# Weight differences in w_out: rows loaded from GpSimd's queue with longer leads, operations and stores one step apart

## The chip, the cores and the metric

The kernel runs on one core of one Trainium2 chip. A core has TensorE (PE: matmuls, into PSUM), VectorE (DVE), ScalarE (ACT) and GpSimd (POOL), and SyncE (SP), which here only issues transfers. ScalarE and GpSimd can issue transfers too; each of the three has a queue of its own, and an instruction that stands in an engine's stream holds up what comes behind it there. The metric is the device time of one execution in microseconds, as the median of the runs taken.

## The reference

One layer of a hybrid encoder, for a prompt of 2048 tokens and a batch of 8 x 16 sampled tokens. Cut to what matters:

```
h   = rms_norm(x, norm_g[0])
z   = h @ w_in                                  # 1024 -> 3592, split among the heads
att = rms_norm(band_attention(qa, ka, va), g_att)
mls = mlstm(qb, kb, vb, ib, fb) * sigmoid(ob)
mix = concatenate([att, mls], -1) @ w_out       # 1024 -> 1024
x   = x + rms_norm(mix, norm_g[1])
u   = rms_norm(x, norm_g[2]) @ w_up             # 1024 -> 5632
y   = conv3(u) ; gate, up = split(y, 2)
x   = x + rms_norm((gelu(gate) * up) @ w_down, norm_g[3])   # 2816 -> 1024
```

The outputs are both x, the attention's keys and values, the mLSTM state and the convolution's last rows. Everything is float32.

## The kernel before, in words

A float32 product is made of three matmuls over a high and a low part of both operands (`mm3`, L104 to L108). The two FFN products are done by a seven-product scheme for 2 x 2 blocks in place of eight: besides the blocks of a weight it needs sums and differences of them. For w_down these are the weight differences of this change. w_down is laid out as 11 units of 128 x 2048 (`NK` = 11), and a unit holds four blocks of 512 columns, called rows 0 to 3 here (the blocks B11, B12, B22, B21). `folds` (L1176) turns each unit into four differences and stores them to the DRAM tensor `wtd`, from which the FFN reads them later (L1379):

```
row 0 = row 1 - row 0
row 1 = row 2 - row 1
row 2 = row 0 - row 2      # of the new row 0
row 3 = row 3 + row 2      # of the new row 2
```

Each is one VectorE operation on 128 x 512 float32 values, in place in one of six slots of the pool `spare` (L58, L71). A new unit's rows take slots that rows of an earlier unit leave, so their load has to wait until the stores of those have landed.

The stages follow one another: projections by w_in with attention and mLSTM worked in between, then the w_out stage (`project`, L976), then the FFN. The w_out stage goes over 17 tiles of 128 tokens: prompt tiles 0 to 7, the sampled tokens, prompt tiles 8 to 15. The last attention and mLSTM units are still worked off beside tiles 0 to 7; from tile 8 on the first FFN rows are prepared (`h2_units`, L1077: square, rsqrt, scale, transpose), and at the end the first up-projection weights are loaded and differenced (L1336 to L1343). Per tile there are:

- `load` of the mixed row `mr` (SP), `norm`: square on ScalarE (L997), then `att_ms` and `att_rs` on GpSimd (L89, L95: mean square and its power -0.5), then scaling on VectorE (L999);
- `turn_rows`: eight transposes on TensorE into `mT_pt`, a rounded high part by ScalarE (L212) and the remainder by VectorE (L213), both into `mt`;
- two halves of 512 columns, each of 24 matmuls into `wo`, evacuated by VectorE (L1033, into `mx`) and ScalarE (L1035, sum of squares), with `wssq` after the first half and `n_ms`, `n_rs` after the second on GpSimd, then the residual on VectorE (L1045) and its store on SP (L1046).

`folds` is a generator that `project` calls after every fourth k of a half (L1026 to L1030): four calls a tile, 68 in all. A unit takes six. In its first call, the loads of rows 0 and 1 are issued from ScalarE's queue (L1188); in the third those of rows 2 and 3 (L1193); the fourth to sixth make the first three operations (L1203); the first call of the next unit makes the fourth (L1208) and issues all four stores from GpSimd's queue (L1210).

The order on each engine is drawn up by the framework's list scheduler, which runs the traced program against a timeline of its own. `keep_in_program_order`, which wraps every load, operation and store of `folds`, puts an instruction behind the one traced just before it on the same engine; instructions that are not wrapped, the FFN's among them, may be drawn ahead of it or behind.

Of the kernel before, what the change touches and what calls it, by code (L numbers as in the profile page):

```python
# [38 lines left out]
HALF = [384, 384, 320]  # L39
PAIRS = [[(((b[j], 0), (b[j + 3], 0)), j * P, P, f"{b[j]}") for j in range(3)] for b in FBLOCKS[:2]]  # L40
NK = NF // 2
UPS = []
WOUT_FOLDS = [("T", k) for k in range(NK)] + [("U", f) for f in UPS]
FAST = (0, 1, 2)
ORDERS = [[f for k in range(NK) for f in (k, k + NK)] if b in FAST else list(range(NF)) for b in range(3)]
B11, B12, B22, B21 = range(4)
# [5 lines left out]
def hymba_step(ctx: ExitStack, tc: tile.TileContext, I: dict, O: dict):  # L52
    nc = tc.nc
# [8 lines left out]
    def ps_mm(name):  # L62
        return psum.tile([P, 512], F32, tag="mm", name=name)
# [7 lines left out]
    def spare_tile(name):  # L71
        return spare.tile([P, 512], F32, tag="k", name=name)

    def dt_(shape, name):
        return dram.tile(shape, F32, tag=name, name=name)
# [12 lines left out]
    def mean_square(ms, ssq, n, eps=EPS):  # L88
        nc.gpsimd.tensor_scalar(ms, ssq, 1.0 / n, eps, op0=ALU.mult, op1=ALU.add)  # L89

    def rsqrt_mean(ssq, n, name, eps=EPS):
        ms = small.tile([P, 1], F32, tag="ms", name=name + "_ms")
        mean_square(ms, ssq, n, eps)
        rs = small.tile([P, 1], F32, tag="rs", name=name + "_rs")
        nc.gpsimd.tensor_tensor(rs, ms, nhalf[:, 0:1], op=ALU.pow)  # L95
        return rs
# [30 lines left out]
    wtd = [dt_([P, 2048], f"wtd{k}") for k in range(NK)]  # L127
    wsd = [dt_([P, 2048], f"wsd{f}") for f in range(NF)]
# [3 lines left out]
    def x_src(t):  # L132
        return I["x_sample"] if t == SAMPLE else I["x_prompt"][t * P:(t + 1) * P, :]
# [84 lines left out]
    def rows_tile(tag, shape, name, dtype=F32):  # L218
        if tag == "xr":
            return rows.tile(shape, dtype, tag="xr", name=name, bufs=2)  # L220
        return pa.tile(shape, dtype, tag=tag, name=name, bufs=1)
# [750 lines left out]
    def drain():  # L972
        while any([p_.step() for p_ in pipes]):
            pass

    def project(tiles):  # L976

        ss = [SimpleNamespace(t=t) for t in tiles]

        def load(s):  # L980
            t = s.t
            if t == 8:
                drain()
                open_ffn()
            s.m = rows_tile("xr", [P, D], f"mr{t}")
            if t == SAMPLE:
                for b in range(DB):
                    own = bass.AP(atts[b].tensor, atts[b].offset, [[512, DS], [DS * 512 + DA, HA], [1, DA]])
                    nc.sync.dma_start(s.m[b * DS:(b + 1) * DS, 0:512].rearrange("p (h d) -> p h d", h=HA), own)
                nc.sync.dma_start(s.m[:, 512:D], mixs)  # L990
            else:
                nc.sync.dma_start(s.m, mixd[t // 4][:, t % 4, :])

        def norm(s):
            mt = wpool.tile([P, 2112], F32R, tag="wh", name=f"mt{s.t}", bufs=2)
            ssq = small.tile([P, 1], F32, tag="ssq", name=f"assq{s.t}")
            nc.scalar.activation(mt[:, :512], s.m[:, :512], AF.Square, accum_out=ssq)  # L997
            rs = rsqrt_mean(ssq, 512, f"att{s.t}")
            nc.vector.tensor_scalar(s.m[:, :512], s.m[:, :512], rs, None, op0=ALU.mult)  # L999
            s.mt = mt[:, :2 * D].rearrange("p (a k n) -> p a k n", a=2, k=KT)  # L1000

        def turn_rows(s):
            rows_to_T(s.m, s.mt, 0, f"mT{s.t}", ps_mm if s.t < 8 else ps_big)

        fold, owed = folds(WOUT_FOLDS), [0.0]
        load(ss[0])
        norm(ss[0])
        yield 0.0, 0.3
        turn_rows(ss[0])
        load(ss[1])  # L1010
        yield 0.9, 1.2
        for n_, s in enumerate(ss):
            t = s.t
            nxt = ss[n_ + 1] if n_ + 1 < len(ss) else None
            if nxt:
                norm(nxt)
            mx = wpool.tile([P, 2112], F32, tag="wl", name=f"mx{t}", bufs=2)
            m, xr = mx[:, 0:D], mx[:, D:2 * D]
            nc.sync.dma_start(xr, x_src(t))
            for hf in range(2):  # L1020
                c = slice(hf * 512, hf * 512 + 512)
                acc = ps_mm(f"wo{t}_{hf}")
                for k in range(KT):
                    mm3(acc, s.mt[:, 0, k, :], s.mt[:, 1, k, :], wo[k][0][:, c], wo[k][1][:, c],
                        start=(k == 0), stop=(k == KT - 1))
                    if k % 4 == 3:  # L1026
                        owed[0] += 6 * len(WOUT_FOLDS) / 66
                        while owed[0] >= 1:
                            owed[0] -= 1
                            next(fold, None)  # L1030
                        yield 2.6, 0.5
                ssq = small.tile([P, 1], F32, tag="wssq", name=f"wssq{t}_{hf}")
                nc.vector.tensor_tensor(m[:, c], acc, g1[0][:, c], op=ALU.mult)  # L1033
                idle = m[:, 512:D] if hf == 0 else s.mt[:, 0, 0:4, :].rearrange("p k n -> p (k n)")
                nc.scalar.activation(idle, acc, AF.Square, accum_out=ssq)  # L1035
                if hf == 0:
                    ssa = ssq
                    mean_square(ssa, ssq, D)
                    if nxt:
                        turn_rows(nxt)  # L1040
                        if n_ + 2 < len(ss):
                            load(ss[n_ + 2])
                        yield 0.9, 1.2
            rs = rsqrt_mean(ssq, D, f"n1_{t}", ssa)
            nc.vector.scalar_tensor_tensor(xr, m, rs, xr, op0=ALU.mult, op1=ALU.add)  # L1045
            nc.sync.dma_start(x2d[t], xr)  # L1046
        for _ in fold:
            pass
# [8 lines left out]
    def open_ffn():  # L1057

        p1.close()
        ffn.p3 = ctx.enter_context(tc.tile_pool(name="p3", bufs=2, reuse_waits="tile"))  # L1060
        ffn.halo = ffn.p3.tile([P, 44, 2], F32, tag="halo", name="halo", bufs=1)
        nc.vector.memset(ffn.halo, 0.0)
        ffn.g2 = ffn.p3.tile([P, D], F32, tag="g2", name="g2", bufs=1)
        nc.sync.dma_start(ffn.g2, I["norm_g"][2:3, :].broadcast_to([P, D]))
        pipes[:] = [Pipe(h2_units(0, lead=6)), Pipe(iter([]))]
# [107 lines left out]
            nc.scalar.copy(hi, lo.bitcast(F32))  # L1173
            nc.vector.tensor_tensor(lo, lo.bitcast(F32), hi, op=ALU.subtract)

    def folds(units):  # L1176

        keep = tc.keep_in_program_order
        sub, plus = ALU.subtract, ALU.add
        ahead = None  # L1180
        for n_, (what, k) in enumerate(units):
            src, dst = (I["w_down"], wtd) if what == "T" else (I["w_up"], wsd)
            part = lambda d, x: d[k][:, x * 512:(x + 1) * 512]
            if ahead:
                ahead()
            q = [spare_tile(f"fold{what}{k}_{x}") for x in range(2)]
            for x in range(2):
                keep(nc.scalar.dma_start(q[x], part(src, x)))  # L1188
            yield
            yield  # L1190
            q += [spare_tile(f"fold{what}{k}_{x}") for x in (2, 3)]
            for x in (2, 3):
                keep(nc.scalar.dma_start(q[x], part(src, x)))  # L1193
            yield
            a, b, c, d = q
            if what == "T":
                ops = [(a, b, a, sub), (b, c, b, sub), (c, a, c, sub), (d, d, c, plus)]
                out = [a, b, c, d]
            else:
                ops = [(c, d, c, plus), (d, a, d, sub), (a, c, a, sub), (b, b, a, sub)]  # L1200
                out = [a, d, c, b]
            for o, x, y, op in ops[:3]:
                keep(nc.vector.tensor_tensor(o, x, y, op=op))  # L1203
                yield

            def ahead(out=out, dst=dst, k=k, last=ops[3]):
                o, x, y, op = last
                keep(nc.vector.tensor_tensor(o, x, y, op=op))  # L1208
                for i, t in enumerate(out):
                    keep(nc.gpsimd.dma_start(dst[k][:, i * 512:(i + 1) * 512], t))  # L1210
        ahead()

    GROUPS = ["va0", "qk0", "qk1", "va1", "qk2", "qk3", "qb0", "vo0", "qb1", "vo1", "qb2", "vo2", "qb3", "vo3"]
    SRC = {g: i for i, g in enumerate(["va0", "qk0", "qk1", "va1", "qk2", "qk3",
# [45 lines left out]
    for n_, (half, gi) in enumerate(seq):  # L1260
        wh, wl, _ = pend
# [5 lines left out]
        i = int(g[2])  # L1267
# [15 lines left out]
        if n_ == len(seq) - 1:  # L1283
            out = project([0, 1, 2, 3, 4, 5, 6, 7, SAMPLE, 8, 9, 10, 11, 12, 13, 14, 15])
# [3 lines left out]
        for u, (pe, dve) in enumerate(it):  # L1288
            ahead = []
# [191 lines left out]
    for b, tiles in enumerate(FBLOCKS):  # L1481
        last = b == len(FBLOCKS) - 1
# [136 lines left out]
        for fi, f in enumerate(ORDERS[b]):  # L1619
# [11 lines left out]
            a, d_, ec = ps_mm(f"ua{nm}"), ps_sm(f"ub{nm}"), ps_big(f"uec{nm}")  # L1631
            e, c = ec[:, 0:512], ec[:, 512:1024]
# [49 lines left out]
        ahead = Pipe(iter([]) if last else h2_units(b + 1, lead=2))  # L1682
        res = {}
        if fast:
# [96 lines left out]
            for p, (_, _, set_, onto) in enumerate(SEQUENCE):  # L1781
                for c in range(3):
# [19 lines left out]
                    for k in range(4 * c, min(4 * c + 4, NK)):  # L1802
                        i = 6 * p + k // 2
# [22 lines left out]
        for dh in range(2):  # L1826
# [56 lines left out]
            out = {j: evacuate(b, j, accs[j], dh) for j in order}  # L1883
# [113 lines left out]
```

## Time and profile before

| | |
|---|---|
| median of 3 runs | 2769.61 us |
| lowest and highest | 2769.04 and 2775.64 us |
| the profiled execution | 2760.67 us, of which its span 2759.0 us |
| mean granted TensorE clock | 0.994 |
| w_out stage, first to last w_out matmul | 1058.7 to 1337.2 us |
| bytes moved | 557.04 MB, mean 202 GB/s |

In the profile, a line such as L1210 is that of the kernel's text. PE is matmuls, PEld the loads of their stationary operand, which overlap. ACTq, SPq and POOLq are the engines' instruction streams where a transfer is issued or a semaphore waited for. A wait is told as "engine, tile, line <- who released it", with the total in us, the number of times and the longest. A row of the timeline has the start in us from the span's start, the duration, the instruction, and in brackets the idle time before it. A row of busy time by stretches has the stretch, its length, the busy us of each engine with its instructions, the granted clock, the DMA engines' busy share and GB/s.

### The profile page before, as it was taken

The numbers are of one execution on the slowest core, as the hardware profiler recorded it, in microseconds if no ns is written. First come the engines' busy times: TensorE is split into PE (matmuls) and PEld (weight loads), VectorE is DVE, ScalarE is ACT, GpSimd is POOL, SyncE is SP. The second block draws the span as 40 slices with busy tenths as digits, with TensorE's granted clock in tenths as the row PEclk, the third lists the DMA queues.
The fourth block names the chain that finished last, engine by engine and source line by source line (L and its number), as shares of the span: only waits on it lengthen the run. The fifth ranks groups of instructions, "written<-read, shape, count | busy, mean of one in ns | idle before, by whom it ended". The sixth has DMA issues, their size and how long they took to land.

```text
span 2759.0 us, 47858 instructions
## 1 busy us (share of the span) xinstructions
PE 2676.8 (97%) x16323; PEld 2506.6 (91%) x16323; DVE 1923.1 (70%) x3643; ACT 1458.3 (53%) x2961; POOL 695.8 (25%) x1353
## 2 busy tenths in 40 slices
PE   7999999999999998999899999999999999999998
PEld 7899999998899997877799997789999878999976
DVE  5344455646446567756799998758888876899966
ACT  4355545635346666533455556654554665555654
POOL 1000010211100002233355542023443212455401
PEclk9999999999999999999999999999999999999999
DMA  5534355547564456568866668767886777789885
GB/s 183 160 116 139 106 160 163 170 149 213 158 190 137 136 173 217 189 221 269 281 202 199 204 203 265 248 199 203 240 240 192 245 236 244 213 257 256 248 270 183
DMA packets 339987, 557.04 MB, mean 202 GB/s; under 512 B 62082, under 2 KB 168414, under 8 KB 339614
## 3 DMA queue, kind: packets, MB, share of 16 engines
q1 hardware_dynamic: 252846, 400.31, 47.0%
q0 software_dynamic: 41968, 108.30, 13.3%
q10 hardware_dynamic: 44928, 45.37, 5.1%
q8 instruction: 128, 2.10, 0.3%
q14 instruction: 117, 0.96, 0.1%
HBM read 389.77 MB, written 173.49 MB: 204 GB/s over the span
## 4 chain that ended last, share of the span: by engine, by line
PE 42%; DVE 4%; DMA 4%; issue 2%; ACT 1%; POOL 1%; DVEq 0%; SPq 0%; POOLq 0%; ACTq 0%
PE uec L106 5%; PE uec L107 5%; PE uec L108 5%; PE dn L108 3%; PE dn L106 3%; PE dn L107 3%; PE ua L108 3%; PE ua L106 2%; PE ua L107 2%; PE dnm L108 1%; PE dnm L107 1%; PE dnm L106 1%; PE ub L108 1%; PE ub L107 1%; PE ub L106 1%
## 5 line engine op out<-in xcount | busy, mean ns | idle before, releaser
L106 PE MATMUL uec<-B,wuh 128*128 128x384 f32 (+1 forms) x720 | 236.2, 328 | 5.7 <-DVE uu L1660 3.5
L107 PE MATMUL uec<-B,wuh 128*128 128x384 f32 (+1 forms) x720 | 235.4, 327 | 0.0
L108 PE MATMUL uec<-B,wul 128*128 128x384 f32 (+1 forms) x720 | 234.7, 327 | 0.0
L1324 ACT CAST wuh<-wu 128x512 fp32r<-128x512 f32 x255 | 141.6, 618 | 109.0 <-PE uec L107 107.6
L108 PE MATMUL dn<-wdh,al 128*128 128x512 f32 x462 | 185.3, 401 | 4.7 <-DVE al L1325 4.5
L1325 DVE TENSOR_TENSOR al<-ar,ah 128x768 fp32r<-128x768 f32 (+2 forms) x141 | 108.6, 780 | 116.0 <-ACT ah L1324 114.5
L106 PE MATMUL dn<-wdh,ah 128*128 128x512 f32 x462 | 183.0, 396 | 4.6 <-ACT ah L1324 2.9
L107 PE MATMUL dn<-wdl,ah 128*128 128x512 f32 x462 | 182.1, 394 | 0.0
L1324 ACT CAST ah<-ar 128x768 fp32r<-128x768 f32 (+2 forms) x141 | 96.2, 692 | 149.9 <-PE dnm L107 110.8
L1325 DVE TENSOR_TENSOR wul<-wu,wuh 128x512 fp32r<-128x512 f32 x255 | 164.5, 685 | 2.4 <-ACT wuh L1324 2.4
L407 DVE CUSTOM_DVE_ANT_0 tmp<-s,nb 128x640 f32<-128x640 f32 (+4 forms) x128 | 94.5, 738 | 94.0 <-PE s L397 92.5
L106 PE MATMUL vo<-wi_h,hT 128*128 128x256 f32 x544 | 155.6, 286 | 0.6 <-DVE mt L213 0.6
L108 PE MATMUL vo<-wi_h,hT 128*128 128x256 f32 x544 | 156.0, 287 | 0.0
L107 PE MATMUL vo<-wi_l,hT 128*128 128x256 f32 x544 | 155.2, 285 | 0.0
L1325 DVE TENSOR_TENSOR wdl<-wdr,wdh 128x512 fp32r<-128x512 f32 x231 | 145.4, 685 | 8.0 <-ACT wdh L1324 5.9
L106 PEld LDWEIGHTS uec<-B,wuh 128*128 128x128 f32 x720 | 135.3, 188 | 8.5 <-DVE uu L1660 4.3
L420 DVE TENSOR_TENSOR ptl<-pt,pth 128x640 fp32r<-128x640 f32 (+4 forms) x128 | 93.9, 738 | 60.8 <-ACT pth L419 59.8
L107 PEld LDWEIGHTS uec<-B,wuh 128*128 128x128 f32 x720 | 135.4, 188 | 0.2
L108 PEld LDWEIGHTS uec<-B,wul 128*128 128x128 f32 x720 | 135.4, 188 | 0.0
L1324 ACT CAST wdh<-wdr 128x512 fp32r<-128x512 f32 x231 | 127.4, 620 | 11.4 <-PE uec L107 7.3
L106 PE MATMUL qk<-hT,wi_h 128*128 128x384 f32 (+1 forms) x384 | 129.6, 337 | 3.6 <-ACT qk_st L238 2.8
L408 ACT ACTIVATE tmp<-tmp,mn 128x640 f32<-128x640 f32 (+4 forms) x128 | 97.6, 763 | 65.9 <-DVE mn L407 64.5
(426 smaller groups left out, 9227.8 us busy)
## 6 DMA issues: line engine op xcount, KB each, us to landing
wu<-in_w_up SPq DMA_DIRECT2D x220, 256.0 KB, 4.9
wu<-wsd SPq DMA_DIRECT2D x176, 256.0 KB, 5.0
wdr<-wtd SPq DMA_DIRECT2D x132, 256.0 KB, 4.8
wi_raw<-in_w_in SPq DMA_DIRECT2D x52, 512.0 KB, 4.0
wdr<-in_w_down SPq DMA_DIRECT2D x99, 256.0 KB, 4.7
wsd<-ws POOLq DMA_DIRECT2D x88, 256.0 KB, 4.8
ar<-ad_S SPq DMA_DIRECT2D x50, 384.0 KB, 5.5
kraw<-kTd SPq DMA_DIRECT2D x112, 128.0 KB, 3.0
```

Of the source, the lines that this page charges most:

```text
L106: nc.tensor.matmul(out, ah, bh, start=start, stop=False, skip_group_check=onto)
L107: nc.tensor.matmul(out, ah, bl, start=False, stop=False, skip_group_check=onto)
L108: nc.tensor.matmul(out, al, bh, start=False, stop=stop, skip_group_check=onto)
L407: nc.vector.tensor_tensor_reduce(o_, s_, b_, 1.0, 3e38, ALU.add, ALU.min, accum_out=mn)
L408: nc.scalar.activation(tmp[:, :n], tmp[:, :n], AF.Exp, bias=mn, scale=-1.0, accum_out=rsum[:, i % 4, hh:hh + 1])
L420: nc.vector.tensor_tensor(s.ptl[:, sl, qc], ptv, s.pth[:, sl, qc], op=ALU.subtract)
L1324: nc.scalar.copy(h, r)
L1325: nc.vector.tensor_tensor(l, r, h, op=ALU.subtract)
```

## The change

Loads are issued from GpSimd's queue instead of ScalarE's. The order within a unit becomes: loads of rows 0 and 1 in the unit's first call, of rows 2 and 3 in the fourth, the first and second operation in the fifth and sixth; the third operation in the next unit's first call, ahead of that unit's loads; stores of rows 0 and 1, then the fourth operation, in its second; stores of rows 2 and 3 in its third. The rate stays one call after every fourth k (`FOLD_RATE` = 1.0; 6 x 11 / 66 before). The branch for differences of w_up, which had no units, goes.

```diff
--- before.py
+++ after.py
@@ -39,8 +39,7 @@
 HALF = [384, 384, 320]
 PAIRS = [[(((b[j], 0), (b[j + 3], 0)), j * P, P, f"{b[j]}") for j in range(3)] for b in FBLOCKS[:2]]
 NK = NF // 2
-UPS = []
-WOUT_FOLDS = [("T", k) for k in range(NK)] + [("U", f) for f in UPS]
+FOLD_RATE = 1.0
 FAST = (0, 1, 2)
 ORDERS = [[f for k in range(NK) for f in (k, k + NK)] if b in FAST else list(range(NF)) for b in range(3)]
 B11, B12, B22, B21 = range(4)
@@ -1002,7 +1001,7 @@
         def turn_rows(s):
             rows_to_T(s.m, s.mt, 0, f"mT{s.t}", ps_mm if s.t < 8 else ps_big)
 
-        fold, owed = folds(WOUT_FOLDS), [0.0]
+        fold, owed = folds(), [0.0]
         load(ss[0])
         norm(ss[0])
         yield 0.0, 0.3
@@ -1024,7 +1023,7 @@
                     mm3(acc, s.mt[:, 0, k, :], s.mt[:, 1, k, :], wo[k][0][:, c], wo[k][1][:, c],
                         start=(k == 0), stop=(k == KT - 1))
                     if k % 4 == 3:
-                        owed[0] += 6 * len(WOUT_FOLDS) / 66
+                        owed[0] += FOLD_RATE
                         while owed[0] >= 1:
                             owed[0] -= 1
                             next(fold, None)
@@ -1173,42 +1172,46 @@
             nc.scalar.copy(hi, lo.bitcast(F32))
             nc.vector.tensor_tensor(lo, lo.bitcast(F32), hi, op=ALU.subtract)
 
-    def folds(units):
+    def folds():
 
         keep = tc.keep_in_program_order
         sub, plus = ALU.subtract, ALU.add
-        ahead = None
-        for n_, (what, k) in enumerate(units):
-            src, dst = (I["w_down"], wtd) if what == "T" else (I["w_up"], wsd)
-            part = lambda d, x: d[k][:, x * 512:(x + 1) * 512]
-            if ahead:
-                ahead()
-            q = [spare_tile(f"fold{what}{k}_{x}") for x in range(2)]
-            for x in range(2):
-                keep(nc.scalar.dma_start(q[x], part(src, x)))
+        live = {}
+
+        def load(k, xs):
+            for x in xs:
+                live[k, x] = spare_tile(f"fold{k}_{x}")
+                keep(nc.gpsimd.dma_start(live[k, x], I["w_down"][k][:, x * 512:(x + 1) * 512]))
+
+        def make(k, o, x, y, op):
+            keep(nc.vector.tensor_tensor(live[k, o], live[k, x], live[k, y], op=op))
+
+        def store(k, xs):
+            for x in xs:
+                keep(nc.gpsimd.dma_start(wtd[k][:, x * 512:(x + 1) * 512], live.pop((k, x))))
+
+        for k in range(NK + 1):
+            now, old = k < NK, k > 0
+            if old:
+                make(k - 1, 2, 0, 2, sub)
+            if now:
+                load(k, (0, 1))
             yield
+            if old:
+                store(k - 1, (0, 1))
+                make(k - 1, 3, 3, 2, plus)
             yield
-            q += [spare_tile(f"fold{what}{k}_{x}") for x in (2, 3)]
-            for x in (2, 3):
-                keep(nc.scalar.dma_start(q[x], part(src, x)))
+            if old:
+                store(k - 1, (2, 3))
             yield
-            a, b, c, d = q
-            if what == "T":
-                ops = [(a, b, a, sub), (b, c, b, sub), (c, a, c, sub), (d, d, c, plus)]
-                out = [a, b, c, d]
-            else:
-                ops = [(c, d, c, plus), (d, a, d, sub), (a, c, a, sub), (b, b, a, sub)]
-                out = [a, d, c, b]
-            for o, x, y, op in ops[:3]:
-                keep(nc.vector.tensor_tensor(o, x, y, op=op))
-                yield
-
-            def ahead(out=out, dst=dst, k=k, last=ops[3]):
-                o, x, y, op = last
-                keep(nc.vector.tensor_tensor(o, x, y, op=op))
-                for i, t in enumerate(out):
-                    keep(nc.gpsimd.dma_start(dst[k][:, i * 512:(i + 1) * 512], t))
-        ahead()
+            if not now:
+                break
+            load(k, (2, 3))
+            yield
+            make(k, 0, 1, 0, sub)
+            yield
+            make(k, 1, 2, 1, sub)
+            yield
 
     GROUPS = ["va0", "qk0", "qk1", "va1", "qk2", "qk3", "qb0", "vo0", "qb1", "vo1", "qb2", "vo2", "qb3", "vo3"]
     SRC = {g: i for i, g in enumerate(["va0", "qk0", "qk1", "va1", "qk2", "qk3",
```

## The prediction

> **What bounds the kernel now.** I read the page's busy shares first, then busy time by stretches, then the waits of the one stage that the change touches, then single tiles there. The first two lines of the page:
>
> ```profile
> span 2759.0 us, 47858 instructions
> ...
> PE 2676.8 (97%) x16323; PEld 2506.6 (91%) x16323; DVE 1923.1 (70%) x3643; ACT 1458.3 (53%) x2961; POOL 695.8 (25%) x1353
> ```
>
> TensorE is the bound: busy 2676.8 of 2759.0 us, so an edit off TensorE can give back at most the 82.2 us in which it idles, and only idle time that the edit's own work causes. The w_out stage runs from the first w_out matmul at 1058.7 us to the last at 1337.2. Busy time in it, in its second part (tiles 8 to 15, no attention left) and in a stretch near its end; columns are PE, PEld, DVE, ACT, POOL, then granted clock, DMA share, GB/s:
>
> ```profile
> 1058.70:1337.20 278.50, 260.44 (x1367) 217.31 (x1367) 178.07 (x326) 124.08 (x299) 84.50 (x162) 0.98 0.70 226
> 1202.00:1337.00 135.00, 122.48 (x567) 97.92 (x566) 76.31 (x103) 47.26 (x98) 46.00 (x87) 0.96 0.82 269
> 1306.00:1321.00 15.00, 11.36 (x53) 8.90 (x52) 4.15 (x7) 3.01 (x7) 5.07 (x9) 0.99 0.91 279
> ```
>
> TensorE idles 278.5 - 260.4 = 18.1 us here, 0.65% of the time: the ceiling of any gain in this stage. GpSimd is busy 30% of it, ScalarE 45%, VectorE 64%. What TensorE waited for between 1080 and 1345 us (total, times, longest):
>
> ```profile
> PE wo L108 <- DVE mt L213: 7.8, 2, 7.3
> PE ot L432 <- ACT pth L419: 3.5, 1, 3.5
> PE h2T_pt L1115 <- DVE x2r L1107: 3.1, 2, 2.9
> ```
>
> No row names a weight difference: the three largest waits are for the split of a transposed tile, an attention probability and a normalised FFN row. The difference tiles themselves (durations ns min/median/max, then first and last start):
>
> ```profile
> L1210 POOL DMA_DIRECT2D wtd<-foldT x44: 539/542/769, 1087.2 to 1335.1; - x44
> L1203 DVE TENSOR_TENSOR foldT<-foldT,foldT x33: 674/684/694, 1086.2 to 1329.6; 128x512 f32<-128x512 f32 x33
> L1188 ACTq DMA_DIRECT2D foldT<-in_w_down x22: 334/354/1647, 1049.1 to 1307.2; - x22
> L1193 ACTq DMA_DIRECT2D foldT<-in_w_down x22: 334/335/566, 1064.3 to 1317.3; - x22
> L1208 DVE TENSOR_TENSOR foldT<-foldT,foldT x11: 627/683/689, 1100.4 to 1332.1; 128x512 f32<-128x512 f32 x11
> ...
>   DMA foldT<-in_w_down: 0.4, 1
> ...
> DMA to landing us min/median/max: 2.6/5.2/10.6
> ```
>
> VectorE waited for a loaded row once, 0.4 us. The result has no hurry either; its first reader comes 367 us after the last store:
>
> ```profile
> L1379 SPq DMA_DIRECT2D wdr<-wtd x132: 319/320/1306, 1702.9 to 2720.8; - x132
> ```
>
> **The change part by part.** Counts stay: 44 loads, 44 VectorE operations, 44 stores. The generator is called 68 times in the stage (17 tiles, two halves, two calls each), every 278.5 / 68 = 4.1 us on average; the last 38 calls, from the sixth unit's first load on, fall into the 135 us of the second row above, one every 3.6 us. I reckon with the shorter step.
>
> *The loads leave ScalarE.* 44 issues of 0.334 to 0.354 us, 15 us of its queue, and this wait for a slot whose store had not landed; beside it stand TensorE's largest wait on ScalarE and the queue's own waits for a slot:
>
> ```profile
> ACT mx L1035 <- DMA wtd<-foldT: 5.0, 1, 5.0
> ...
> 1084.83 0.38 PE L432 MATMUL ot<-pth,vhl 128*128 128x256 f32 x1 [3.47 <-ACT pth L419]
> ...
> L1193 ACTq EVENT_SEMAPHORE  x14: 17/17/17, 1097.5 to 1316.8; - x14
> ```
>
> ScalarE idles 154 of 278.5 us, and TensorE's largest wait on it, 3.5 us, ends at 1084.8, before the first wait for a slot at 1097.5, so it cannot come from one. On the path: 0.
>
> *The loads come to GpSimd.* There is no row for such a load; the nearest is the store, 0.542 us. 44 x 0.542 = 23.8 us, which takes GpSimd from 84.5 to 108 of 278.5 us. As time it is hidden by GpSimd's idle 194 us; as delay it stands ahead of the small rsqrt operations (att_ms, att_rs, n_ms, n_rs) that gate the normalised rows. A pair puts 1.1 us in front of them. The slack is read at a late tile, in order of time on GpSimd, VectorE, TensorE:
>
> ```profile
> 1309.10 0.55 POOL L95 TENSOR_TENSOR att_rs<-att_ms,nhalf 128x1 f32<-128x1 f32 x1
> 1309.60 2.29 POOL L1210 DMA_DIRECT2D wtd<-foldT  x4
> ...
> 1309.68 0.49 DVE L999 TENSOR_SCALAR mr<-mr,att_rs 128x512 f32<-128x512 f32 x1 [0.71 <-POOL att_rs L95]
> ...
> 1313.99 1.03 PE L78 MATMUL mT_pt<-ident,mr 128*128 128x128 f32 x8
> ```
>
> The row is normalised at 1310.17 and transposed at 1313.99: 3.8 us cover one or two issues. Cost 0; without that cover 1.1 us a pair, 22 pairs, 24 us at the very most. How long the load itself takes from issue to landing:
>
> ```profile
> foldT<-in_w_down ACTq DMA_DIRECT2D x44, 256.0 KB, 5.8
> wtd<-foldT POOLq DMA_DIRECT2D x44, 256.0 KB, 5.2
> ```
>
> GpSimd's queue is not slower for 256 KB, so the nearest estimate for the load is 5.2 to 5.8 us. By the Trainium skill, DMA: Bandwidth & Descriptors, section Specifications, a DMA from GpSimd delivers its first byte after about 1 us and one from ScalarE after about 0.6: by that each load would land 0.4 us later, an estimate that the two medians here do not show (they differ the other way, load against store).
>
> *The leads.* Rows 0 and 1 are used four calls after their load instead of three, 14.4 against 10.8 us; row 2 stays at two calls (7.2 us), row 3 at four. Against a landing of 5.2 to 5.8 us all have cover, and the wait that could go is the 0.4 us shown. If a load is late all the same, VectorE stands, and behind it the evacuation L1033; but that one waits itself:
>
> ```profile
> DVE mx L1033 <- PE wo L108: 26.8, 10, 5.3
> ```
>
> So 0. Bounds: -0.4, and on the other side row 2 of all 11 units landing at the longest, 10.6 - 7.2 = 3.4 us late, 37.4 us of VectorE, of which 26.8 it stands idle today: +10.6.
>
> *Operations and stores one call apart.* VectorE does the same 0.684 us each. The stores no longer stand in one burst of four behind the last operation, so these waits of GpSimd's queue go:
>
> ```profile
> POOL wtd L1210 <- DVE foldT L1203: 5.5, 3, 3.2
> POOL wtd L1210 <- DVE foldT L1208: 4.8, 4, 2.8
> POOL wtd L1210 <- DVE ad L657: 2.5, 1, 2.5
> ```
>
> 12.8 us of GpSimd standing, none of which reaches a row of TensorE's waits: 0. In exchange, GpSimd's own loads of rows 2 and 3 must wait until the store of the previous unit's rows 0 and 1 has landed, a wait that ScalarE carried so far. What stands behind it is the same rsqrt chain. Two calls (7.2 us) lie between, against a median landing of 5.2: 0 at the median. The other end is the second rival.
>
> *The end.* The last two operations slip one call, the last into the final half tile, and the last pair of stores (1.1 us) behind the stage. The closing evacuation waits for TensorE anyway:
>
> ```profile
> 1337.11 0.69 DVE L1033 TENSOR_TENSOR mx<-wo,norm_row 128x512 f32<-128x512 f32 x1 [4.38 <-PE wo L108]
> ```
>
> 4.4 us of idle cover 0.68: 0, or +0.7 at most without it.
>
> *The 7.3 us stall.* It arises where four FFN differences (L1341) stand before the split L213 on VectorE and their input lands late, with the DMA share at 0.91:
>
> ```profile
> 1308.83 1.07 SPq L1336 DMA_DIRECT2D wu<-in_w_up  x1
> ...
> 1320.88 0.69 DVE L1341 TENSOR_TENSOR ws<-wu,wu 128x512 f32<-128x512 f32 x1 [9.51 <-DMA wu<-in_w_up]
> ...
> 1323.42 1.22 DVE L213 TENSOR_TENSOR mt<-mT_pt,mt 128x1024 fp32r<-128x1024 f32 x1
> ...
> 1324.69 0.79 PE L108 MATMUL wo<-wo,mt 128*128 128x512 f32 x1 [7.33 <-DVE mt L213]
> ```
>
> The differences' traffic crosses that load: four stores at 1309.6 and loads on either side. After the change a pair of stores (0.52 MB, 1.9 us at 279 GB/s) comes a little later, and the pair of loads of that unit comes later too, behind att_rs: -1.9 to +1.9, and I take 0, since the bytes stay.
>
> **Sum.** 0 on the path. The profiled execution took 2760.67 us, its span 2759.0 and 1.67 around it; the median of the runs shown, 2769.61, lies 8.94 above it. So 2760.7 + 0 + 8.9 = 2769.6.
>
> **Rivals.** *B, the tail untangles (faster).* The order on each engine is drawn up by the framework's list scheduler on its own estimate of time, and a moved difference can shift the FFN work among the tiles. If L213 comes ahead of L1341, and the h2T transposes a few matmuls later, 7.3 + 2.9 = 10.2 us go: 2759.4. For: both stalls are orders that the data did not keep. Against: nothing edited is one of the instructions concerned.
>
> *C, GpSimd stands for its slots (slower).* Pinned only behind the previous GpSimd instruction, the four issues can run up close to one another: store pair, store pair, load pair. Then the load waits the store's landing less three issues, and the rsqrt chain stands behind it. It decides from the point where that hold passes the 3.8 us of slack. In the later seven units the transfers of these tiles land so:
>
> ```profile
> DMA to landing us min/median/max: 3.4/6.2/10.6
> ```
>
> A median store holds 6.2 - 1.6 = 4.6 us, 0.8 beyond the slack; the longest 9.0, 5.2 beyond. Two of the seven at the longest and five at the median: 10.4 + 4.0 = 14.4, so 2784.0. For: 82% DMA share there. Against: in the trace of before GpSimd stood 12.8 us for stores without a trace on TensorE.
>
> *D, the leads do not grow.* Issue order, not the call, sets when a queue gets to a load; behind att_rs or wssq the extra call may vanish. Waits move by tenths: 2769.6, as forecast.
>
> *E, GpSimd's issue is held by VectorE.* The longest GpSimd issue of any kind is an accumulating one:
>
> ```profile
> L1446 POOL DMA_DIRECT2D x2d<-f x24: 865/892/2075, 1908.3 to 2534.0; - x24
> ```
>
> If each load took 2.08 instead of 0.54 us, a pair would come 3.1 us later, and ten holds at C's all-stage median (5.2 - 1.6 = 3.6) would reach 6.7, 2.9 over the slack: +29, 2798.6. By the Trainium skill, SBUF — State Buffer, section SBUF: two separate sides, GpSimd cannot write descriptors while VectorE holds the port pair that both share. The 44 stores, at 769 ns at most beside a VectorE 64% busy, speak against it.
>
> **Numbers.** Forecast 0.46, B 0.20, C 0.21, D 0.10, E 0.03. About 0.3% (8.3 us) is what a measurement of this kernel can tell from no change: faster 0.20 (B), slower 0.24 (C and E), same 0.56. The forecast's own range is 2767 to 2778 (the tail's 1.9 and the leads' 0.4 about the runs shown, 2769.04 to 2775.64). The full range goes from 2756, B with the wait of 3.5 for pth reordered away too, to 2786, C with the tail's 1.9; the leads' +10.6 lies inside. Outside are E and about a third of C and of B, 0.17.
>
> **What would show it.** Right: 44 loads from GpSimd near 0.54 us each, ScalarE's 5.0 us slot wait gone, TensorE's idle time in the stage near 18 us, with L213 and x2r still its largest releasers. B: the 7.3 us row missing. C: GpSimd's loads idling on stores of wtd, and TensorE waiting on a chain that ends in att_rs. E: a load's issue well over 1 us. The forecast falls if TensorE's idle time changes by more than 8 us in this stage, or at all in the FFN, whose instructions the change does not touch.

## The result, and the profile after

| | before | after |
|---|---|---|
| median of six runs each | 2770.92 us | 2757.14 us |
| lowest to highest | 2765.86 to 2775.64 us | 2753.62 to 2764.04 us |
| the profiled execution | 2760.67 us | 2753.91 us |

The ratio of after to before is 0.9955, with a 95% interval of 0.9942 to 0.9969: the change makes the kernel 0.45% faster, some 12 us. The forecast, no change, did not come: the time lies below its own range (2767 to 2778), inside the full range (2756 to 2786), and near that of rival B (2759.4).

The first two lines of the page of after:

```profile
span 2752.2 us, 47852 instructions
...
PE 2677.0 (97%) x16323; PEld 2504.0 (91%) x16323; DVE 1922.8 (70%) x3643; ACT 1457.1 (53%) x2961; POOL 731.5 (27%) x1397
```

Over the whole execution TensorE is busy as long as before, 2677.0 against 2676.8 us. The w_out stage shows what went: first the kernel before, from the first to the last w_out matmul and in a stretch near the end, then the same stage after. Both stage rows hold the same matmuls, 1413 of them. The columns are the stretch, its length, the busy us of PE, PEld, DVE, ACT and POOL, the granted clock, DMA share and GB/s:

```profile
1050.30:1337.00 286.70, 267.55 (x1413) 223.47 (x1412) 184.36 (x340) 129.78 (x312) 86.27 (x165) 0.98 0.71 229
1320.80:1327.60 6.80, 2.91 (x7) 2.33 (x8) 4.92 (x7) 1.70 (x4) 2.98 (x6) 0.50 0.88 269
```

```profile
1049.20:1321.10 271.90, 263.43 (x1413) 219.63 (x1412) 184.25 (x341) 130.05 (x314) 113.64 (x207) 1.00 0.74 241
```

The stage is 14.8 us shorter. TensorE idles 8.5 us in it instead of 19.2, which makes 10.7; the same matmuls take 4.1 us less. The granted clock of before is 0.50 in three places of the stage: for 3.4 us from 1085.3 and from 1221.8, and for 6.8 from 1320.8, each at one of the three waits that the prediction shows. After, it is full all through the stage. TensorE's waits of after in the stage (total, times, longest):

```profile
PE pt L77 <- DVE ptl L419: 1.7, 1, 1.7
PE h2T_pt L1114 <- DVE x2r L1106: 1.6, 2, 0.9
...
PE wo L107 <- DVE mt L212: 0.4, 1, 0.4
```

The three largest waits of before are gone or short: 7.3 us for the split of a transposed tile (L213) is 0.4, 3.5 for an attention probability (L419) is 0.3, and 2.9 for a normalised FFN row (L1107) is 0.9 (the line numbers of after are lower by one up to `folds`, and higher by three behind it). From the first w_out matmul to the first of the down projection, the profiled executions took 611.3 us before and 599.8 after, 11.5 less: 3.3 of the stage's 14.8 us are lost again between its end and that point (324.6 and 327.9 us). (The first w_out matmul of before is at 1050.3 us; the 1058.7 given ahead of the prediction is a later one.) Behind that point every engine has the same instructions in the same order in both kernels. It took 1097.4 and 1103.2 us; that 5.8 the other way is spread between executions, and it is why the profiled pair differs by 6.8 us only.

**The first place: the tail of the stage.** The timeline of before, rows beside those that the prediction shows:

```profile
1306.09 1.58 SPq L1336 DMA_DIRECT2D wu<-in_w_up  x3
1306.76 0.37 ACTq L1188 DMA_DIRECT2D foldT<-in_w_down  x1
1307.22 0.41 ACTq L1188 DMA_DIRECT2D foldT<-in_w_down  x1
...
1325.28 0.63 PE L106 MATMUL wo<-wo,mt 128*128 128x512 f32 x1
1325.71 0.63 PE L107 MATMUL wo<-wo,mt 128*128 128x512 f32 x1
```

And the timeline of after:

```profile
1298.42 1.59 SPq L1339 DMA_DIRECT2D wu<-in_w_up  x3
...
1300.68 0.62 SPq L1339 DMA_DIRECT2D wu<-in_w_up  x1
...
1301.49 0.55 POOL L94 TENSOR_TENSOR att_rs<-att_ms,nhalf 128x1 f32<-128x1 f32 x1
1301.99 1.32 POOL L1184 DMA_DIRECT2D fold<-in_w_down  x2
1303.30 1.08 POOL L1191 DMA_DIRECT2D wtd<-fold  x2
...
1306.31 0.69 DVE L1344 TENSOR_TENSOR ws<-wu,wu 128x512 f32<-128x512 f32 x1 [1.82 <-DMA wu<-in_w_up]
...
1310.46 0.40 PE L105 MATMUL wo<-wo,mt 128*128 128x512 f32 x1
```

The FFN's first differences (ws) need four blocks of w_up, loaded by SyncE three and one. Before, ScalarE sends two 256 KB loads for the differences of w_down beside the second and the third, ahead of the fourth, and ws starts 12.05 us after the fourth was issued (1308.83, 1320.88). After, GpSimd sends the same two loads behind att_rs, 1.3 us after the fourth, and ws starts 5.63 us after it. VectorE waits 1.82 instead of 9.51 us for it. ws still stands before the split on VectorE: the order was not mended, its input came sooner. TensorE's 7.33 us becomes 0.39. Behind the long stall its matmuls also started 0.43 us apart instead of 0.23, some 1.2 us in all over the seven starts up to 1327.76. This place is worth 7.33 - 0.39 + 1.2 = 8.1 us.

What the DMA engines moved from the issue of the fourth block to ws, before and then after (q1 is SyncE's queue, q10 ScalarE's, q0 GpSimd's; packets, MB, share of the engines' time):

```profile
DMA packets 2039, 3.74 MB, mean 309 GB/s; under 512 B 210, under 2 KB 722, under 8 KB 2039
...
q1 hardware_dynamic: 1382, 2.07, 52.2%
q0 software_dynamic: 320, 1.05, 23.4%
q10 hardware_dynamic: 337, 0.62, 21.4%
```

```profile
DMA packets 1163, 1.64 MB, mean 294 GB/s; under 512 B 82, under 2 KB 594, under 8 KB 1162
...
q1 hardware_dynamic: 1156, 1.61, 92.8%
q0 software_dynamic: 6, 0.02, 1.1%
```

The rate is about the same; the bytes are not. Before, the pair and all four stores of differences (1.05 MB, issued 0.8 us and more behind the block) were moved before ws could start; after, next to nothing of either. The trace does not tell how much of the delay is the stores' doing.

**The second place: 1084 us.** ScalarE's stream before and after:

```profile
1082.60 0.42 ACT L662 ACTIVATE mvo<-mvo 128x256 f32<-128x256 f32 x1 [2.04 <-DMA mvo<-vobd]
...
1083.35 0.33 ACTq L1188 DMA_DIRECT2D foldT<-in_w_down  x1
1083.51 0.67 ACT L419 CAST pth<-pt 128x640 fp32r<-128x640 f32 x1
```

```profile
1076.40 1.29 ACT L418 CAST pth<-pt 128x640 fp32r<-128x640 f32 x2 [0.26 <-PE ot L431]
...
1078.59 0.41 ACT L661 ACTIVATE mvo<-mvo 128x256 f32<-128x256 f32 x1
```

Before, the mLSTM's gate (mvo) stands ahead of the attention's cast (pth) in ScalarE's stream and waits there for its load; TensorE stands 3.47 us for pth. After, pth comes first and TensorE waits 0.3. Here the order on an engine did change, between two instructions that the change does not touch. Worth 3.2 us of idle time in the pair of profiles, and the stretch of half clock behind it.

**The third place: 1222 us.** TensorE's longest wait for a normalised FFN row (x2r) is 2.9 us before and 0.9 after. The row's square on ScalarE waits for the load of x2r there, 4.0 us before and 2.1 after; why that load comes sooner was not looked into. The three places make 12.1 us of idle time; other waits took 1.4 back.

**The differences themselves.** The tile's view in after:

```profile
L1184 POOL DMA_DIRECT2D fold<-in_w_down x44: 543/544/764, 1053.9 to 1312.7; - x44
L1187 DVE TENSOR_TENSOR fold<-fold,fold x44: 628/684/695, 1074.8 to 1321.0; 128x512 f32<-128x512 f32 x44
...
  DMA wtd<-fold: 11.4, 6
  DVE fold L1187: 11.1, 4
  DMA fold<-in_w_down: 3.0, 2
```

GpSimd's load costs 0.544 us, as estimated. VectorE waits 3.0 us for rows instead of 0.4, in spite of the longer leads. GpSimd stands 11.4 us for slots, a wait that ScalarE had.

### The profile page after: what moved, and what is told of

Same layout as the page of the kernel before. It is cut to its first block, busy times and chain, and to the rows that moved or that the text cites. A ratio compares the mean times of both kernels' runs of the same rounds, so it can differ in the third digit from the quotient of the medians.

```text
span 2752.2 us, 47852 instructions
## 1 busy us (share of the span) xinstructions
PE 2677.0 (97%) x16323; PEld 2504.0 (91%) x16323; DVE 1922.8 (70%) x3643; ACT 1457.1 (53%) x2961; POOL 731.5 (27%) x1397
## 3 DMA queue, kind: packets, MB, share of 16 engines
q0 software_dynamic: 45488, 119.84, 14.8%
## 4 chain that ended last, share of the span: by engine, by line
PE 43%; DVE 4%; DMA 3%; issue 1%; ACT 1%; POOL 0%; SPq 0%; DVEq 0%; POOLq 0%; ACTq 0%
PE uec L105 5%; PE uec L106 5%; PE uec L107 5%; PE dn L107 3%; PE dn L105 3%; PE dn L106 3%; PE ua L107 3%; PE ua L106 3%; PE ua L105 3%; PE dnm L107 1%; PE dnm L106 1%; PE ub L107 1%; PE dnm L105 1%; PE ub L105 1%; PE ub L106 1%
## 5 line engine op out<-in xcount | busy, mean ns | idle before, releaser
L419 DVE TENSOR_TENSOR ptl<-pt,pth 128x640 fp32r<-128x640 f32 (+4 forms) x128 | 93.6, 738 | 57.8 <-ACT pth L418 56.9
```

The source lines that it names most:

```text
L419: nc.vector.tensor_tensor(s.ptl[:, sl, qc], ptv, s.pth[:, sl, qc], op=ALU.subtract)
```

## The experiments

All were timed in five rounds against the kernel before on the same chip. The stalls are those of TensorE in one profiled execution of each, and the last column is its stretch from the first w_out matmul to the first of the down projection.

| version | ratio to before | interval | stall at the tail | stall for pth | stretch |
|---|---|---|---|---|---|
| before | 1 | | 7.3 | 3.5 | 611.3 |
| the change | 0.9955 | 0.9942 to 0.9969 | 0.4 | 0.3 | 599.8 |
| e1, change, loads on ScalarE | 0.9986 | 0.9976 to 0.9997 | 7.1 | 2.7 | 611.5 |
| e2, before, loads on GpSimd | 0.9963 | 0.9950 to 0.9976 | 0.4 | 0.3 | 601.8 |
| e3, no differences | 0.9932 | 0.9918 to 0.9946 | none | 0.3 | 588.8 |
| e4, before, 1.2 calls | 1.0015 | 1.0001 to 1.0028 | none | 3.8 | 612.9 |
| f1, change, loads on SyncE | 0.9998 | 0.9986 to 1.0010 | 3.1 | 3.9 | 612.3 |
| g1, before, rows 0, 1 on GpSimd | 0.9955 | 0.9941 to 0.9970 | 0.5 | 2.0 | 603.6 |
| g2, before, rows 2, 3 on GpSimd | 0.9980 | 0.9967 to 0.9992 | 6.7 | 3.7 | 610.5 |
| h1, before, last unit on GpSimd | 0.9961 | 0.9947 to 0.9975 | 0.3 | 3.7 | 602.5 |
| h2, change, last unit on ScalarE | 0.9962 | 0.9948 to 0.9976 | 3.3 | 0.3 | 603.9 |
| i1, before, last rows 0, 1 early | 0.9963 | 0.9949 to 0.9976 | 0.8 | 4.0 | 608.1 |
| j1, before, sixth unit on GpSimd | 0.9989 | 0.9978 to 1.0000 | 7.2 | 3.1 | 610.2 |
| k1, change, rows 2, 3 on ScalarE | 0.9949 | 0.9936 to 0.9961 | 0.5 | 0.3 | 603.2 |

### Which part does it: the queue or the steps

**e1** keeps the new steps and gives the loads back to ScalarE:

```diff
-                keep(nc.gpsimd.dma_start(live[k, x], I["w_down"][k][...]))
+                keep(nc.scalar.dma_start(live[k, x], I["w_down"][k][...]))
```

> The changed kernel with one thing undone: its 44 loads are issued from ScalarE's queue again, at the changed calls. If moving the loads to GpSimd is what gave the time (theory Q: loads off ScalarE's queue), the time goes back to the kernel before, 2768 to 2774 us, and TensorE's 7 us stall before the last tile's split comes back. If the new calls (operations and stores one call apart) gave it (theory S), it stays at 2755 to 2761. If neither, but the list scheduler's order in the stage (theory O), anything from 2750 to 2780 with a different set of waits.

Most of the gain is lost, 0.9986. The timeline of e1 at the tail has the same picture as before:

```profile
1312.63 0.36 ACTq L1184 DMA_DIRECT2D fold<-in_w_down  x1
1313.08 0.40 ACTq L1184 DMA_DIRECT2D fold<-in_w_down  x1
...
1314.87 0.98 SPq L1339 DMA_DIRECT2D wu<-in_w_up  x1
...
1326.50 0.69 DVE L1344 TENSOR_TENSOR ws<-wu,wu 128x512 f32<-128x512 f32 x1 [8.52 <-DMA wu<-in_w_up]
```

The pair goes out ahead of the fourth block and ws starts 11.6 us behind it. The new leads and steps alone are not the gain.

**e2** keeps the old steps and moves the loads only (both `nc.scalar.dma_start` of the old `folds` become `nc.gpsimd.dma_start`).

> The kernel before with one thing done: its 44 loads are issued from GpSimd's queue, at the old calls; stores still in bursts of four. Theory Q: 2755 to 2761 us, as the whole change. Theory S: 2768 to 2774, no gain. Theory O: anything from 2750 to 2780.

0.9963, within the interval of the whole change. What the change brings comes with moving the loads.

**e3** bounds what is to be had: `project` gets an empty generator, and the FFN reads blocks of w_down in place of the differences.

```diff
-        fold, owed = folds(WOUT_FOLDS), [0.0]
+        fold, owed = iter([]), [0.0]
...
-            src = I["w_down"][k] if blk < 4 else wtd[k]
+            src = I["w_down"][k]
```

> The kernel before without the loads, operations and stores of the w_down differences; the FFN reads blocks of w_down in place of the differences, so the outputs that hang on the FFN are not the reference's. It prices the whole of this work on the path. If the differences' traffic is what makes the tail's load land late, TensorE's idle time in the w_out stage falls from 18 us to under 10 and the time to 2755 or below; if the stalls in the stage come from elsewhere, it stays within 8 us of the kernel before.

0.9932, and TensorE idles 2.6 us in the stage: as the first of the two outcomes has it. By the ratios this is 0.23% or 6 us below the change, though the two intervals just touch. All that the differences still cost beside the rest of the stage is about that much; their issue, waits and operations were hidden but for the places above.

**e4** is the kernel before with 1.2 calls where it made one (`owed[0] += 1.2`).

> The kernel before with its differences called 1.2 times as often, so that they are done some 13 calls before the stage ends and cross no up-projection load at its end. If the traffic of the differences beside that load made the 7.3 us stall (theory T), the stall goes and the time falls by 5 to 9 us, 2762 to 2766; by theories Q and S nothing in how the loads are issued changes and it stays at 2768 to 2774.

1.0015. The tail's stall is gone, since the last of the differences is stored at 1303.8 us, ahead of the blocks of w_up, but the 5 to 9 us that theory T gave for it did not come: other stalls stand in its place. TensorE's waits of e4:

```profile
PE mT_pt L78 <- ACT mx L1035: 5.2, 2, 3.6
PE ot L432 <- ACT pth L419: 3.8, 1, 3.8
```

ScalarE also waits 3.2 us for a slot ahead of L212; whether such waits are what makes mx late was not followed up. The faster rate took one stall away and has another.

### Which loads, and the queue or the place in time

The theory from here on: what counts is that two loads of the last unit go out just ahead of the fourth block of w_up, whichever queue sends them (place). Its rival: ScalarE's queue itself is what slows SyncE's (queue).

**f1** is the changed kernel with the loads on SyncE (`nc.sync.dma_start`), where the pair stands in one queue with the blocks of w_up.

> The changed kernel with its 44 loads issued from SyncE's queue. If it is enough that ScalarE no longer issues them (theory Q1: ScalarE's stream, or its second hardware queue beside SyncE's), the time is that of the changed kernel, 0.994 to 0.997 of the kernel before. If it must be GpSimd's queue, because loads there come after SyncE's and leave SyncE's stream free (theory Q2), the slot waits now hold up SyncE's other loads: 0.998 to 1.005.

0.9998: nothing gained. The pair goes out at 1310.74, ahead of all four blocks, the fourth is followed by ws after 7.3 us, and the tail's stall is 3.1 us. By the stalls alone some 4 us of gain were due. The profile tells where they went. TensorE idles 13.7 us in the stage, 5.4 less than before, but the same matmuls take 272.2 us instead of 267.6: the granted clock is 0.96 over the stage, and 0.50 for 6.8 us at each of three places, the stall for pth (3.9 us), two of 1.3 us 2 us apart at 1225, and the tail's. SyncE itself stands 54 us for slots:

```profile
SPq L1184 <- DMA wtd<-fold: 54.0, 18, 6.3
```

**g1** and **g2** move one half of the loads of the kernel before, rows 0 and 1 (the first of the two `dma_start` of a unit) or rows 2 and 3 (the second).

> The kernel before with rows 0 and 1 alone loaded from GpSimd's queue; rows 2 and 3, whose loads wait for slots that the previous unit's stores leave, stay on ScalarE's. If the slot waits in ScalarE's stream are the cost (theory W), nearly nothing is gained: 0.998 to 1.001. If each load that leaves ScalarE's queue gives its share (theory R, the transfers' competition with SyncE's), half of the gain: 0.997 to 0.999; the tail's stall hangs on the loads of rows 0 and 1 of the last unit, so by R it should be smaller.

> The kernel before with rows 2 and 3 alone loaded from GpSimd's queue; rows 0 and 1 stay on ScalarE's. Theory W: the whole gain, 0.995 to 0.997. Theory R: half of it, 0.997 to 0.999, with the tail's 7 us stall still there, since the loads of rows 0 and 1 still run beside the up-projection load.

g1 has the whole gain, 0.9955, more than either theory gave it; g2 keeps the 6.7 us stall and has 0.9980. It is rows 0 and 1.

**h1** moves the last unit only, and **j1**, its control, the sixth only:

```diff
-                keep(nc.scalar.dma_start(q[x], part(src, x)))
+                keep((nc.gpsimd if k == NK - 1 else nc.scalar).dma_start(q[x], part(src, x)))
```

(j1 has `k == NK // 2`.)

> The kernel before with the loads of the last of 11 units alone on GpSimd's queue. If the gain is the tail (theory T: the last unit's loads beside the up-projection load), most of it comes, 0.995 to 0.998, and the 7 us stall goes. If the gain is spread over the stage, 0.998 to 1.001.

> The kernel before with the loads of the sixth unit alone on GpSimd's queue, an edit of the same size as that of the last unit, at a place without a stall. Theory T: 0.999 to 1.001. If any such edit gains by the order that the list scheduler then draws (theory O), 0.995 to 0.998.

Four loads of 44 make the gain: h1 0.9961, j1 0.9989. In h1's timeline the pair comes after the fourth block:

```profile
1308.22 0.58 SPq L1336 DMA_DIRECT2D wu<-in_w_up  x1
...
1311.74 1.08 POOL L1188 DMA_DIRECT2D foldT<-in_w_down  x2
1313.74 0.69 DVE L1341 TENSOR_TENSOR ws<-wu,wu 128x512 f32<-128x512 f32 x1 [2.51 <-DMA wu<-in_w_up]
```

**i1** tells place from queue: every load stays on ScalarE, but rows 0 and 1 of the last unit are loaded three calls earlier.

```diff
+                if k == NK - 2 and n == 0:
+                    early = rows01(k + 1)
...
-            q = [spare_tile(f"fold{what}{k}_{x}") for x in range(2)]
-            for x in range(2):
-                keep(nc.scalar.dma_start(q[x], part(src, x)))
+            q = early or rows01(k)
```

> The kernel before with all loads on ScalarE's queue, but rows 0 and 1 of the last unit loaded three calls earlier, about 10 us, so that they have landed before the first up-projection loads go out. If it is when these two loads run (theory T, place), the gain of the single unit on GpSimd's queue comes here too: 0.995 to 0.998. If it is ScalarE's queue as such (theory Q), 0.998 to 1.001.

0.9963: the gain without GpSimd's queue. The pair is out some ten us before the blocks of w_up, and the timeline has

```profile
1313.75 0.57 SPq L1344 DMA_DIRECT2D wu<-in_w_up  x1
...
1319.72 0.69 DVE L1349 TENSOR_TENSOR ws<-wu,wu 128x512 f32<-128x512 f32 x1 [2.98 <-DMA wu<-in_w_up]
```

In this version, too, four stores of differences go out behind the fourth block, 1.2 us after it (0.8 in the kernel before); ws still starts 6.0 us after it, when only 0.09 MB of them have moved. So the stores alone do not delay the block. Whether the pair would without them, no run shows. The profiled execution of i1 shows less than its median does: its stage is 281.2 us, 5.5 less than before, with 4.0 us for pth and 2.0 for x2r still in it.

**h2**, the reverse, is the changed kernel with the last unit's loads on ScalarE (`nc.scalar if k == NK - 1 else nc.gpsimd`).

> The changed kernel with the loads of the last unit alone back on ScalarE's queue. If the tail is nearly all of the gain (theory T), it is lost again: 0.998 to 1.000 of the kernel before, with the 7 us stall before the last tile's split. If the other ten units give it, 0.994 to 0.997.

A miss in part: 0.9962, most of the gain stays. The pair is between the blocks again, and ws is late, but by less:

```profile
1302.25 0.35 ACTq L1184 DMA_DIRECT2D fold<-in_w_down  x1
1302.72 0.42 ACTq L1184 DMA_DIRECT2D fold<-in_w_down  x1
...
1303.67 1.05 SPq L1339 DMA_DIRECT2D wu<-in_w_up  x1
...
1312.28 0.69 DVE L1344 TENSOR_TENSOR ws<-wu,wu 128x512 f32<-128x512 f32 x1 [4.75 <-DMA wu<-in_w_up]
```

8.6 us from issue to ws, between the 5.5 to 6.0 of the versions without the pair in that place and the 11.4 to 12.1 of before, e1, g2 and j1; TensorE stands 3.3 us. The place costs something here too, but less. The trace has 2.79 MB moved in these 8.6 us, with 0.52 MB of the stores, which the changed kernel sends in two pairs; in the four others it is 3.46 to 3.74 MB, with 1.03 to 1.05. That goes with the delay; since e1 also stores in pairs, it is no proof. The change's 12.5 us less that stall would be a gain of 9; 0.9962 is 10.5.

**k1** is the changed kernel with rows 2 and 3 on ScalarE (`nc.gpsimd if x < 2 else nc.scalar`), the nearest guess at a better version.

> The changed kernel with rows 2 and 3 loaded from ScalarE's queue, rows 0 and 1 from GpSimd's. GpSimd's waits for slots (11.4 us in the changed kernel) go. If they cost TensorE anything, it is faster than the changed kernel, 0.992 to 0.994; by theory T it is the same as that, 0.994 to 0.997, since only rows 0 and 1 of the last unit stand beside the up-projection load.

0.9949, not to be told from the change's 0.9955. No version clearly beats the changed kernel.

### The second stall, read across the runs

No run was made for the stall at pth; it shows by lining up the profiles. In the five with pth ahead of mvo on ScalarE (the change, e2, e3, h2, k1) it is 0.3 us, in the nine with mvo ahead 2.0 to 4.0. What it is worth in time is smaller than these intervals: the versions without the tail's stall but with this one (g1, h1, i1) have 0.9955 to 0.9963, those with neither (the change, e2, k1) 0.9949 to 0.9963. So the tail is shown by runs, the second place by profiles only. So is the third: the longest wait for x2r is 2.9 us before and from nothing to 2.0 in all the others, with the gain or without. Why the scheduler puts pth first in some is open: taking the early loads off ScalarE is not enough (f1), nor is leaving some there fatal (k1).

Also open: e1, g2 and j1, with both stalls, are 0.1 to 0.2% under before, more than the intervals of the first two allow as chance. In their profiles the wait for x2r is 1.1 us at most.

## Why the prediction was right or wrong

- **What bounds.** The stage's gain, 14.8 us, stayed under the ceiling of 18.1, but only 10.7 of it is idle time; 4.1 came out of TensorE's busy time through the clock, for which the prediction had no term. That "no row names a weight difference" was read as their having no part in the largest wait; the row names who released TensorE last, and the load that made the releaser late stood two steps back, in ScalarE's queue.
- **The step that failed: the 7.3 us stall.** "The differences' traffic crosses that load" was right, and i1, h1 and g1 show that it is the pair of loads. The size was wrong: "-1.9 to +1.9, and I take 0, since the bytes stay". The bytes stay in the stage, but not ahead of the block: between its issue and ws 3.74 MB were moved before and 1.64 after, at about the same rate. That took 6.4 us off the way from the block's issue to ws (12.05 to 5.63) and 7.3 - 0.4 off the stall. The prediction even said that the pair "comes later too, behind att_rs"; it priced one pair of transfers, 0.52 MB at 279 GB/s, and not what else would then no longer run ahead of the block. How the 6.4 us divide between the pair and the stores stays open. The half clock behind the stall, 1.2 us, was no term at all.
- **Loads leave ScalarE: 0.** Right for the issues and the 5.0 us slot wait: no row of TensorE's waits answers to them. The argument on pth, that a wait ending at 1084.8 cannot come from a slot wait, was right; that nothing else could move it was not said, and the order did.
- **Loads on GpSimd: 0.** Right: 0.544 us each, GpSimd busy 27% of the span instead of 25.
- **The leads: 0, from -0.4 to +10.6.** Right in value. They did not grow into cover: VectorE's waits rose to 3.0 us. Rival D's point holds, with a time of its own nowhere.
- **Operations and stores: 0; the end: 0.** Right on the path: no row of TensorE's waits names them. But the waits of GpSimd's queue for VectorE's operations, 12.8 us, which were to go, did not: they are 11.1 after.
- **B.** Near in time, and its two stalls did shrink (7.3 to 0.4, 2.9 to 0.9), but not by its reason. It had L213 drawn ahead of L1341 and the h2T transposes a few matmuls later; both orders stayed, and the inputs came sooner. A reordering did come, at pth, which B named only as the low end of the range. So it is in part luck that the full range, whose low end was B's, held the result. "Nothing edited is one of the instructions concerned" was no argument against: list scheduling moved pth and mvo all the same.
- **C.** Its wait came: 11.4 us in six holds, the longest in this row of GpSimd's waits:

```profile
POOL fold L1184 <- DMA wtd<-fold: 11.4, 6, 3.9
```

3.9 us against a slack read as 3.8: it hardly passed the point from which it decides. Of TensorE's waits only one of 0.4 us leads back to att_rs, at 1097.5 us, ahead of the first of these holds (1127). The mean hold, 1.9 us, was well under the 4.6 assumed.

- **E.** No: the longest load issue is 0.764 us beside a VectorE 68% busy in the stage. The Trainium skill, SBUF — State Buffer, section SBUF: two separate sides, has GpSimd's descriptor writing blocked in some VectorE modes; no issue here shows it. Nor do the landings show the later first byte of GpSimd's transfers (the Trainium skill, DMA: Bandwidth & Descriptors, section Specifications): median us to landing in after, from first fold on,

```profile
wtd<-fold POOLq DMA_DIRECT2D x44, 256.0 KB, 6.2
fold<-in_w_down POOLq DMA_DIRECT2D x42, 256.0 KB, 5.4
```

5.4 for the load, where ScalarE's took 5.8.

- **What would show it.** TensorE's idle time in the stage changed by 10.7 us, more than 8, the mark at which the forecast was to fall, and it fell. L213 is no longer among its largest releasers. In the FFN no change shows beyond the spread of executions.

## What to carry to other kernels

A stall whose releaser is a late load is a question about everything issued just ahead of that load, on every queue: look at the two or three microseconds before its issue, and count every byte that is moved until it lands, those of later transfers in other queues too. The mean rate held here; the count of bytes was wrong. Moving background transfers costs or gains by where they land between critical ones, so move the single pair in question (one unit, or the same queue earlier) before crediting the queue. And with a list scheduler an edit that leaves an instruction alone may still move it: compare the order on each engine around the largest waits before a stall is counted as fixed in place.

## What the runs showed of the hardware

- With two loads of 256 KB issued just ahead of it in another queue, a load of 256 KB was used 11.4 to 12.1 us after its issue in four versions and 8.6 in one, against 5.5 to 6.0 without them. At the 279 GB/s of that stretch their own bytes take 1.9 us; 1.05 MB of stores, issued behind that load from a further queue, were moved before its use too. In the kernel before, the DMA engines moved little just then, though they were busy; the stretches around the fourth block's issue, with the columns as above:

```profile
1306.00:1309.00 3.00, 3.00 (x14) 2.40 (x14) 2.34 (x3) 1.30 (x4) 2.08 (x3) 1.00 0.66 147
1309.00:1312.00 3.00, 3.00 (x15) 2.40 (x14) 1.69 (x3) 0.55 (x2) 2.81 (x6) 1.00 0.78 162
1312.00:1315.00 3.00, 3.00 (x19) 2.54 (x18) 0.00 (x0) 0.14 (x2) 0.19 (x1) 1.00 1.05 374
```

  147 and 162 GB/s, then 374. Why they were slow is open; it is not the pair alone, since after, without it, 1300 to 1302 us has 137 GB/s.
- A stall of TensorE costs more than its length: after 7.3 us the next matmuls took 0.63 us and started 0.43 apart, and 0.40 and 0.23 later; in h2 the same followed a stall of 3.3 us. The granted clock is 0.50 over those matmuls. The Trainium skill, TensorE: Matmul & The Clock Gate, section Why this matters for your kernels, puts the drop of the clock at some 3 us of idle. These two agree, and after 0.4 us in the changed kernel none is seen; but the clock was also 0.50 behind stalls of 2.0 us (g1, twice) and 2.2 (k1), each with shorter ones of up to 0.5 near it, and at the two of 1.3 in f1; behind single ones of 1.7 (after, e4) it stayed full. So less than 3 us was enough here.
- Executions of one kernel spread by up to 19 us (0.7%, g1), so that a pair of profiles (6.8 us here) did not show a difference of medians of 13.8 us; the stretch of the changed stage alone did.
